# A hybrid decoder layer: the first SSD chunk is transposed by matmuls, and the probabilities of the last four head pairs by VectorE and DRAM

## The chip, the core and the metric

The kernel runs on one core of one Trainium2 chip. Five engines run side by side, each through its own instructions in order: PE (TensorE, matmuls; PEld is its loading of stationary operands), DVE (VectorE), ACT (ScalarE), POOL (GpSimd) and SP (SyncE, which here only starts DMAs). The metric is the device time of one execution in microseconds, as the median of several runs. Before the change it is 1031.97 us (three runs, 1031.74 to 1032.63).

## The reference, cut to what matters

One decoder layer over 512 tokens of width 1024, in float32. The token mixer projects the normalized input once and feeds two branches: attention with a window of 128 and a learned sink per head (16 query heads, 2 key heads), and a state-space scan (SSD) in chunks of 128 tokens (32 heads in 4 groups). Both are projected back, gated, summed and projected again; a SwiGLU block follows.

```python
# attention, in blocks of 128 queries against 256 keys (the block before and its own)
scores = einsum('bnqkgd,bnskd->bnkgqs', qb, k_band)
p = exp(where(valid, scores + bias, -inf) - m)
p = p / (sum(p, -1) + exp(sink - m))
out = einsum('bnkgqs,bnskd->bnqkgd', p, v_band)          # sums over the keys s
# SSD, one chunk c of 128 tokens, group g, head e
X = xh * dt[..., None]                                   # tokens x 64 per head
CB = einsum('bclgn,bcsgn->bcgls', Cc, Bc)
y_diag = einsum('bcgels,bcsgep->bclgep', exp(segsum(dA)) * CB, X)
states = einsum('bclgn,bcgel,bclgep->bcgepn', Bc, decay_states, X)
```

Both last sums run over tokens that the kernel holds along the wrong axis: the probabilities lie as queries x keys and the product with V wants keys on the partitions; x and B come out of the projection as channels x tokens, and the SSD products want tokens on the partitions. So both need 128x128 transposes.

## The kernel before, in words

All large products are made in three passes (`mm3`, lines 149 to 151: high x high, low x high, high x low parts of the operands), 24 matmuls of 128x512 per unit of 128 output columns. A unit's weights are loaded to `w_raw` (SP, line 120, four buffers), rounded to `w_hi` by ACT (line 135) and subtracted to `w_lo` by DVE (line 136), three units ahead; its result is taken out of one of three PSUM accumulators by ACT and DVE.

PE's order is the program's text. The side work (scores, transposes, SSD products) is written between calls of `fill(us)`, each of which lets a list of projection units go on for some steps of three matmuls. For DVE, ACT, POOL and SP the text does not fix the order: a scheduler places their instructions by its own estimate of when each can run, and from then on each engine takes them strictly in turn.

Attention, one pair of heads `t` (0 to 7) after the other. `scores(t+1)` makes the scores (line 436), the bias and mask (441, 443), the maximum (449), eight exps on ACT (461), the sums and reciprocal (463, 464), and POOL multiplies the reciprocal in (466): `sc`, two heads x four blocks of 128x256, of which 128 columns per block are stored, each block's own keys and the past block's sharing one square by the triangle mask. Then `weighted_values(t)` transposes the eight squares on PE (479, into `ps_pt`), and splits each by the triangle: the part at or before the query is `ps_pt` times `tri` on DVE (485), the rest is copied by ACT (481) and masked by POOL (482). Both make `pT`, the moving operand of `ps_o` (492).

The loop over `t` sits at lines 673 to 695. During the last pairs ACT also takes the exps' results on: sigmoids of `tB` (714) and SiLUs of the first group's x, B and C (716), with a table load of the activation function at each turn from one to the other. POOL multiplies and adds the input normalization's weights into four `row` tiles (704, 705) behind the last pair's mask. Then eight units `yb` follow.

SSD, 16 chunks `i` (4 groups x 4). `ssd_pre` loads the cumulative sums `L` by a broadcasting DMA, POOL masks them (756) and ACT takes 8 exps (761). `ssd_x` transposes x and B in squares of 32 on DVE (770, 781), writes them to DRAM (`t_d`, `b_d`) and reads them back with the squares in their places (`R`, `bt`; SP, lines 774 to 786). `ssd_dt` multiplies dt in: `X` on DVE (797), `Xd` on POOL (805). `ssd_a` makes C x B (822), copies it (824) and multiplies it into `L` (826). `ssd_b` makes the state `ps_st` (836), then `ps_yo` and `ps_yd` (862). Ahead of the loop stand `ssd_pre` of two chunks and the transposes of two; in it each step prepares the chunks after.

## Time and profile before

| | us |
|---|---|
| median of the runs shown | 1031.97 |
| the profiled execution | 1031.27 |
| its span, first to last instruction | 1029.5 |
| PE busy | 1008.2 (98% of the span) |
| DVE, ACT, POOL busy | 616.8, 499.2, 207.4 |
| largest wait of PE in one place | 10.0 |

An engine's line gives its busy time; the rows of 40 slices give it in tenths per slice of 25.7 us, and PEclk is the clock granted to TensorE. A timeline row gives start, length, engine, line, operation, output <- inputs, shape and count, and in brackets how long the engine stood idle before it and what ended that. A row of the chain of waits gives start, length and what ran. Matmuls of one stream overlap: 0.39 us is one's length, about 0.23 us the distance from one to the next.

### The profile page before, as it was taken

Reading aid. Unit: us, or ns where it says so; the run is one execution under the profiler, and the core shown is the slowest. Engines: PE = TensorE matmul, PEld = TensorE weight load, DVE = VectorE, ACT = ScalarE, POOL = GpSimd, SP = SyncE. Lnnn points to the kernel's source line nnn. Section 1 sums busy time; section 2 is a strip of 40 time slices with the busy share of each in tenths; the row PEclk is TensorE's granted clock in tenths of the full one; section 3 lists DMA queues with packets and bytes.
Section 4 is the critical chain, followed back from the end, with each engine's and each line's share of the span. In section 5 each row is a group of like instructions: output and inputs, shape, how many; then the busy total and the mean of one; then the engine's idle time right before and its main releaser. Section 6 shows DMA issues by size and latency. Waiting matters only on the chain.

```text
span 1029.5 us, 13358 instructions
## 1 busy us (share of the span) xinstructions
PE 1008.2 (98%) x4968; PEld 830.0 (81%) x4968; DVE 616.8 (60%) x911; ACT 499.2 (48%) x848; POOL 207.4 (20%) x195
## 2 busy tenths in 40 slices
PE   8999999996999999999999999999999999999997
PEld 7888888884887887888888888898888888888886
DVE  6789874545655785696874585646433333332766
ACT  5464566716555786684652543334323332322441
POOL 2011223722204113212322820290000000000000
PEclk9999999998999999999999999999999999999999
DMA  8211223545554445445532344316433333331471
GB/s 316 82 62 62 88 83 106 198 146 148 171 156 146 153 153 151 125 142 159 166 113 83 115 150 180 107 42 225 144 122 114 111 111 114 123 123 62 147 251 53
DMA packets 58961, 136.53 MB, mean 133 GB/s; under 512 B 12912, under 2 KB 23152, under 8 KB 58640
## 3 DMA queue, kind: packets, MB, share of 16 engines
q1 hardware_dynamic: 56240, 126.11, 37.9%
q0 software_dynamic: 2080, 7.47, 2.0%
q10 hardware_dynamic: 576, 2.10, 0.5%
q8 instruction: 39, 0.64, 0.3%
q14 instruction: 26, 0.21, 0.1%
HBM read 124.25 MB, written 11.40 MB: 132 GB/s over the span
## 4 chain that ended last, share of the span: by engine, by line
PE 88%; DVE 4%; ACT 3%; DMA 3%; issue 1%; POOL 1%; SPq 0%; ACTq 0%; POOLq 0%; DVEq 0%
PE ps_mm L149 13%; PE ps_mm L150 13%; PE ps_mm L151 13%; PE ps_ff L151 8%; PE ps_ff L149 8%; PE ps_ff L150 8%; PE ps_da L151 2%; PE ps_da L149 2%; PE ps_da L150 2%; PE ps_db L150 2%; PE ps_db L151 2%; PE ps_db L149 2%; PE ps_mix L149 1%; PE ps_mix L151 1%; PE ps_mix L150 1%; DMA L<-a_d 1%
## 5 line engine op out<-in xcount | busy, mean ns | idle before, releaser
L136 DVE TENSOR_TENSOR w_lo<-w_raw,w_hi 128x1024 fp32r<-128x1024 f32 x185 | 241.3, 1309 | 171.1 <-ACT w_hi L135 169.0
L135 ACT CAST w_hi<-w_raw 128x1024 fp32r<-128x1024 f32 x185 | 193.6, 1050 | 307.9 <-PE ps_ff L150 124.4
L149 PE MATMUL ps_mm<-hT_hi,w_hi 128*128 128x512 f32 x504 | 204.3, 405 | 0.7 <-DVE cacc L373 0.7
L150 PE MATMUL ps_mm<-hT_lo,w_hi 128*128 128x512 f32 x504 | 197.2, 391 | 0.0
L151 PE MATMUL ps_mm<-hT_hi,w_lo 128*128 128x512 f32 x504 | 197.0, 391 | 0.0
L149 PE MATMUL ps_ff<-h2T_hi,w_hi 128*128 128x512 f32 (+1 forms) x384 | 143.3, 373 | 0.0
L151 PE MATMUL ps_ff<-h2T_hi,w_lo 128*128 128x512 f32 (+1 forms) x384 | 142.6, 371 | 0.0
L150 PE MATMUL ps_ff<-h2T_lo,w_hi 128*128 128x512 f32 (+1 forms) x384 | 142.6, 371 | 0.0
L149 PEld LDWEIGHTS ps_mm<-hT_hi,w_hi 128*128 128x128 f32 x504 | 95.0, 188 | 23.2 <-issue 4.2
L151 PEld LDWEIGHTS ps_mm<-hT_hi,w_lo 128*128 128x128 f32 x504 | 94.8, 188 | 20.6
L150 PEld LDWEIGHTS ps_mm<-hT_lo,w_hi 128*128 128x128 f32 x504 | 95.1, 189 | 18.7 <-issue 1.2
L150 PEld LDWEIGHTS ps_ff<-h2T_lo,w_hi 128*128 128x128 f32 x384 | 72.3, 188 | 12.6
L151 PEld LDWEIGHTS ps_ff<-h2T_hi,w_lo 128*128 128x128 f32 x384 | 72.3, 188 | 12.5
L149 PEld LDWEIGHTS ps_ff<-h2T_hi,w_hi 128*128 128x128 f32 x384 | 72.3, 188 | 12.4
L1152 DVE TENSOR_TENSOR sgf<-sgf,ps_ff 128x512 f32<-128x512 f32 x22 | 15.1, 685 | 68.3 <-PE ps_ff L151 68.3
L149 PE MATMUL ps_mm<-yh,w_hi 128*128 128x512 f32 x124 | 49.4, 399 | 0.3 <-ACT yacc L934 0.3
L150 PE MATMUL ps_mm<-yl,w_hi 128*128 128x512 f32 x124 | 48.4, 390 | 0.0
L151 PE MATMUL ps_mm<-yh,w_lo 128*128 128x512 f32 x124 | 48.3, 390 | 0.0
L756 POOL TENSOR_SCALAR_AFFINE_SELECT L<-L 128x1024 f32<-128x1024 f32 x16 | 21.8, 1360 | 118.2 <-DMA L<-a_d 92.5
L761 ACT ACTIVATE L<-L,nac 128x128 f32<-128x128 f32 x128 | 40.1, 390 | 6.9 <-POOL L L756 6.6
L373 DVE SCALAR_TENSOR_TENSOR cacc<-ps_mm,pc,cacc 128x511 f32<-128x511 f32 (+2 forms) x54 | 39.6, 737 | 6.2 <-ACT cacc L370 5.7
L150 PE MATMUL ps_da<-w_lo,hA_hi 128*128 128x512 f32 x88 | 34.2, 389 | 0.0
(264 smaller groups left out, 1675.4 us busy)
## 6 DMA issues: line engine op xcount, KB each, us to landing
w_raw<-in_wall_dram SPq DMA_DIRECT2D x187, 512.0 KB, 3.4
L<-a_d SPq DMA_DIRECT2D x16, 512.0 KB, 5.9
t_d<-T SPq DMA_DIRECT2D x16, 256.0 KB, 3.9
R<-t_d SPq DMA_DIRECT2D x64, 64.0 KB, 2.0
E<-e_d SPq DMA_DIRECT2D x24, 128.0 KB, 3.5
x_d<-x_sb POOLq DMA_DIRECT2D x4, 512.0 KB, 7.8
row<-x_d POOLq DMA_DIRECT2D x4, 512.0 KB, 5.1
h_d<-row POOLq DMA_DIRECT2D x4, 512.0 KB, 3.0
```

The source lines that it names most:

```text
L135: (copy or nc.scalar.copy)(out=hi, in_=w)
L136: self.last = (eng or nc.vector).tensor_sub(out=lo, in0=w, in1=hi.bitcast(F32))
L149: nc.tensor.matmul(ps, lh, rh, start=start, stop=False)
L150: nc.tensor.matmul(ps, lh, rl, start=False, stop=False)
L151: nc.tensor.matmul(ps, ll, rh, start=False, stop=stop)
L373: nc.vector.scalar_tensor_tensor(out=acc[:, d:], in0=ps[:, :S - d], scalar=pc[:, cw + 3 - d:cw + 4 - d], in1=acc[:, d:], op0=ALU.mult, op1 ...
L756: nc.gpsimd.affine_select(out=Lf, in_=Lf, pattern=[[0, 8], [1, P]], compare_op=ALU.is_ge, fill=-BIG, base=0, channel_multiplier=-1)
L761: nc.scalar.activation(L[:, j, t], L[:, j, t], AF.Exp, bias=nac5[:, g, j, c, t:t + 1], scale=1.0)
L1152: nc.vector.tensor_mul(sg, sg, pu)
```

## The change

For the pairs 4 to 7 the eight transposes on PE go away. Instead DVE transposes in squares of 32 into `Tp`, one DMA writes 512 KB to DRAM (`p_d`), four DMAs of 128 KB read it back into the place of `sc`, and POOL and DVE multiply by `past` and `tri` into `pT`; ACT's copies for these pairs go away too. The writing half is issued behind `scores(t+1)`, the multiplications stand two yields ahead of `ps_o`. For the first SSD chunk the way over DRAM goes away: PE transposes x (`ps_x`) and B (`ps_bt`), `X` is made from `ps_x` in PSUM, and ACT copies `ps_bt`.

```diff
+    p_d = dram.tile([NQ, P, 4, 2 * P], F32, name="p_d")
...
+    def transposed_p(t):
+
+        sc = att_p[t]
+        T = Tp
+        if not back_t:
+            nc.gpsimd.tensor_sub(past, ones, tri)
+        for j in range(2):
+            nc.vector.transpose(
+                T[:, :, NT * j:NT * j + NT].rearrange("p b m s -> p m b s"),
+                sc[:, j].rearrange("p m (b s) -> p m b s", b=4))
+        nc.sync.dma_start(out=p_d[t], in_=T.rearrange("p b m s -> p b (m s)"))
+        back = sc.rearrange("p j n k -> p (j n k)").rearrange("p (a x) -> p a x", a=4)
+        for b in range(4):
+            nc.sync.dma_start(
+                out=back[32 * b:32 * b + 32], in_=p_d[t, :, b].rearrange("(a r) x -> r a x", r=32))
+        back_t[t] = back.rearrange("p a (m s) -> p m a s", s=32)
...
     def weighted_values(t):
...
-        for j in range(2):
+        if t in back_t:
+            yield
+            for j in range(2):
+                own = back_t[t][:, NT * j:NT * j + NT]
+                last_sel[0] = nc.gpsimd.tensor_tensor(
+                    out=pT[:, j, 1::2].rearrange("p n (a s) -> p n a s", a=4), in0=own[:, 1:],
+                    in1=past.rearrange("p (a s) -> p a s", a=4).unsqueeze(1).broadcast_to([P, NT - 1, 4, 32]),
+                    op=ALU.mult)
+                nc.vector.tensor_tensor(
+                    out=pT[:, j, 0::2].rearrange("p n (a s) -> p n a s", a=4), in0=own,
+                    in1=tri.rearrange("p (a s) -> p a s", a=4).unsqueeze(1).broadcast_to([P, NT, 4, 32]),
+                    op=ALU.mult)
+            yield
+        for j in range(0 if t in back_t else 2):
             ps = axt([P, NT, P], "ps_pt")
...
+    past = at.tile([P, P], F32, name="past")
+    Tp = at.tile([P, 4, 2 * NT, 32], F32, name="Tp")
...
             next(s1)
+            if t + 1 >= NQ // 2:
+                transposed_p(t + 1)
...
+    def ssd_first():
+
+        ps = axt([P, 4, P], "ps_x")
+        for t in range(4):
+            nc.tensor.transpose(ps[:, t], xbc_t[0, 2 + t][:, 0:P], ident)
+        R_t[0] = ps.rearrange("p t (a s) -> p a t s", a=4)
+        ps = axt([P, P], "ps_bt")
+        nc.tensor.transpose(ps, xbc_t[0, 0][:, 0:P], ident)
+        bt_t[0] = sd.tile([P, P], F32, name="bt", tag="bt", bufs=2)
+        nc.scalar.copy(out=bt_t[0], in_=ps)
...
     ssd_pre(0)
     ssd_pre(1)
-    ssd_x(0)
     ssd_a(0)
-    fill(4.0)
+    ssd_first()
     ssd_dt(0)
     ssd_x(1)
+    fill(4.0)
```

The list of units is empty at both places of `fill(4.0)` (the units of the SSD stage are added inside the loop), so moving it moves nothing.

The scheduled engines change order at three places. First, DVE at the last pair, from its sums to the end of its output. Before:

```order
L463 TENSOR_TENSOR sm<-sm,es 128x8
L464 RECIPROCAL sm<-sm 128x8
L136 TENSOR_TENSOR w_lo<-w_raw,w_hi 128x1024
L231 TENSOR_TENSOR attT_lo<-ps_o,attT_hi 128x512
L136 TENSOR_TENSOR w_lo<-w_raw,w_hi 128x1024
L485 TENSOR_TENSOR pT<-ps_pt,tri 128x4x128 x2
L136 TENSOR_TENSOR w_lo<-w_raw,w_hi 128x1024
L231 TENSOR_TENSOR attT_lo<-ps_o,attT_hi 128x512
```

And now:

```order
L464 TENSOR_TENSOR sm<-sm,es 128x8
L465 RECIPROCAL sm<-sm 128x8
L136 TENSOR_TENSOR w_lo<-w_raw,w_hi 128x1024
L481 STREAM_TRANSPOSE Tp<-sc 128x4x4x32 x2
L231 TENSOR_TENSOR attT_lo<-ps_o,attT_hi 128x512
L136 TENSOR_TENSOR w_lo<-w_raw,w_hi 128x1024 x2
L504 TENSOR_TENSOR pT<-sc,tri 128x4x128 x2
L231 TENSOR_TENSOR attT_lo<-ps_o,attT_hi 128x512
```

The two multiplications into `pT` stood behind the second `w_lo` after the reciprocal; now they stand behind the third.

Second, ACT in the same stretch, from the copy behind the last pair's exps to the `w_hi` that belongs to that third `w_lo`. Before:

```order
L411 COPY tB<-ps_mm 128x512
L135 CAST w_hi<-w_raw 128x1024
L714 ACT_TABLE_LOAD
L714 ACTIVATE tB<-tB 128x512
L481 COPY pT<-ps_pt 128x3x128 x2
L716 ACT_TABLE_LOAD
L716 ACTIVATE bc_f<-bc_f 128x512
L411 COPY tB<-ps_mm 128x512
L135 CAST w_hi<-w_raw 128x1024
```

And now:

```order
L135 CAST w_hi<-w_raw 128x1024
L412 COPY tB<-ps_mm 128x512
L754 ACT_TABLE_LOAD
L754 ACTIVATE bc_f<-bc_f 128x512
L752 ACT_TABLE_LOAD
L752 ACTIVATE tB<-tB 128x512
L754 ACT_TABLE_LOAD
L754 ACTIVATE bc_f<-bc_f 128x512
L412 COPY tB<-ps_mm 128x512
L135 CAST w_hi<-w_raw 128x1024
```

The two copies into `pT` are gone; the first `w_hi` has moved ahead of a table load and a SiLU that came before it; the last `w_hi` has the same work ahead of it as before, without the copies.

Third, ACT at the start of SSD. Before:

```order
L824 COPY cb<-ps_cb 128x128 x2
L761 ACT_TABLE_LOAD
L761 ACTIVATE L<-L,nac 128x128 x16
L370 ACTIVATE cacc<-ps_mm,pc 128x512
L135 CAST w_hi<-w_raw 128x1024
L761 ACTIVATE L<-L,nac 128x128 x8
```

And now:

```order
L873 COPY cb<-ps_cb 128x128
L837 COPY bt<-ps_bt 128x128
L873 COPY cb<-ps_cb 128x128
L799 ACT_TABLE_LOAD
L799 ACTIVATE L<-L,nac 128x128 x24
L371 ACTIVATE cacc<-ps_mm,pc 128x512
L135 CAST w_hi<-w_raw 128x1024
L891 COPY h_st<-ps_st 128x512
```

The exps of the third `L` have moved ahead of the first unit's evacuation (`cacc`) and of a `w_hi`.

## The prediction

> **What bounds the kernel now.** I read the page first, then PE's waits, then PE's timeline where it waits. The engines' busy time, and their shares of the chain of waits:

> ```profile
> PE 1008.2 (98%) x4968; PEld 830.0 (81%) x4968; DVE 616.8 (60%) x911; ACT 499.2 (48%) x848; POOL 207.4 (20%) x195
> PE 88%; DVE 4%; ACT 3%; DMA 3%; issue 1%; POOL 1%; SPq 0%; ACTq 0%; POOLq 0%; DVEq 0%
> ```

> PE bounds it: 98% busy, 88% of the chain. The longest of its waits (total, times, longest):

> ```profile
> PE ps_st L836 <- POOL Xd L805: 10.0, 1, 10.0
> ```

> So apart from this one, about half of the 2% that PE idles, only instructions taken off PE can gain, and any new wait of PE costs in full. The change does both, at two places.

> **First place: the start of SSD.** PE's timeline around the wait (start, length), a normal `ps_st` and the transposes' rate from the chain of waits, and the clock by windows (its column is the last but two):

> ```profile
> 244.06 0.39 PE L150 MATMUL ps_mm<-hT_lo,w_hi 128*128 128x512 f32 x1
> 244.28 0.39 PE L151 MATMUL ps_mm<-hT_hi,w_lo 128*128 128x512 f32 x1
> 254.64 2.08 PE L836 MATMUL ps_st<-Xd,bt 128*128 128x512 f32 x2 [9.97 <-POOL Xd L805]
> 258.52 0.40 PE L151 MATMUL ps_mm<-hT_hi,w_lo 128*128 128x512 f32 x1
> 277.46 0.86 PE ps_st L836 x2
> 646.92 0.44 PE ps_tr L217 x4
> 247.00:248.00 1.00, 0.00 (x0) 0.00 (x0) 0.30 (x2) 0.92 (x4) 0.05 (x1) 1.00 0.71 258
> 248.00:249.00 1.00, 0.00 (x0) 0.00 (x0) 1.00 (x2) 1.00 (x5) 0.00 (x0) 0.55 0.45 139
> 258.00:259.00 1.00, 1.00 (x5) 0.76 (x5) 0.00 (x0) 0.00 (x0) 1.00 (x3) 0.83 0.35 84
> ```

> From 244.28 to 258.52 pass 14.24 us. The work in between is one `ps_st` (0.86) and six steps from one matmul to the next (0.23 each), some 2.35 with the turns. So the place costs 11.9: 10 of waiting and 1.9 because the clock fell 3.4 us into the idle time and came back 3.7 us after PE had work. What PE waited for is the chain over DRAM and then a busy DVE:

> ```profile
> 238.05 0.88 DVE L770 STREAM_TRANSPOSE T<-xs_f 128x128 f32<-128x128 f32 x4
> 238.18 2.56 ACT L819 ACTIVATE y_g<-xs_f,pc 128x512 f32<-128x512 f32 x4
> 241.43 5.92 DMA b_d<-Tb
> 252.79 0.75 DVE L797 TENSOR_TENSOR X<-R,dtv 128x256 f32<-128x256 f32 x2
> 253.29 1.30 POOL Xd L805 x2
> ```

> The change removes this way for the first chunk. `X` needs only `ps_x` (PE, right ahead of the fill) and DVE, free at 238.05; two `X` (0.75) and two `Xd` (1.3, ahead of the masks on POOL now) end near 241, `bt` behind ACT's four `y_g` (to 240.7) near 241, and `ps_st` is due at 245. That is four us of cover; gone, each us of it is PE's. Added on PE: five transposes at 0.11, 0.55. **Gain 11.9 - 0.55 = 11.3.**

> What is late next: PE is 11 us earlier against ACT and DVE, and ACT now takes all 24 exps before it empties the first unit's accumulator.

> ```profile
> 251.83 2.45 ACT L761 ACTIVATE L<-L,nac 128x128 f32<-128x128 f32 x8 [0.70 <-POOL L L756]
> 249.44 0.76 ACT L370 ACTIVATE cacc<-ps_mm,pc 128x512 f32<-128x512 f32 x1
> 247.93 1.18 DVE L826 TENSOR_TENSOR L<-L,cb 128x1024 f32<-128x1024 f32 x1
> 249.91 1.89 POOL L756 TENSOR_SCALAR_AFFINE_SELECT L<-L 128x1024 f32<-128x1024 f32 x1 [2.86 <-DMA L<-a_d]
> ```

> The third `L` landed at 249.9; with 256 KB (`t_d` of the first chunk) less ahead of it, moved at about 260 KB per us by the window row above, and an issue earlier (0.3), it lands some 1.3 earlier and the exps, which ended at 254.3, end near 253.0. `cacc` 0.76, then DVE's three additions (0.7 each) with a `w_lo` (1.2, as the product in the third row) among them: free near 257.1. PE wants that accumulator for its fourth unit at 245.1 + 0.9 (`ps_st`) + nine steps of 0.68 + 1.1 (`ps_yd`) + five steps = 256.6. **Loss 0.5**; none if `L` lands 0.5 earlier still, 1.8 if it lands as before. `ps_yd` itself needs the first `L`, whose product ended at 249.1 before: three us of cover.

> **Second place: the transposes off PE.** PE's timeline in pair 5 (`ps_pt` is a group of four transposes):

> ```profile
> 147.00 0.48 PE L149 MATMUL ps_mm<-hT_hi,w_hi 128*128 128x512 f32 x1
> 147.78 0.60 PE L479 MATMUL ps_pt<-ident,sc 128*128 128x128 f32 x4
> 148.14 0.48 PE L149 MATMUL ps_mm<-hT_hi,w_hi 128*128 128x512 f32 x1
> ```

> From step to step pass 1.14 with a group, and three distances, 0.68, without: 0.46 a group, eight groups. **Gain 3.7**, if `pT` is there in time. ACT loses four pairs of copies, off the path.

> The new way of pair 5, by rows: DVE's reciprocal, POOL's `sc`, the write (512 KB as `w_raw`), four reads (`R`'s issue time and landing), the multiplication on DVE, and `ps_o` of pairs 4 and 5; the transposes are in the row at 238.05 (four of 128x128 stand for one half):

> ```profile
> 136.49 0.20 DVE L464 RECIPROCAL sm<-sm 128x8 f32<-128x8 f32 x1
> 136.84 2.04 POOL L466 TENSOR_TENSOR sc<-sc,sm 128x512 f32<-128x512 f32 x2 [3.64 <-DVE sm L464]
> w_raw<-in_wall_dram SPq DMA_DIRECT2D x3, 512.0 KB, 3.3
> 247.47 1.75 SPq L776 DMA_DIRECT2D R<-t_d  x4
> R<-t_d SPq DMA_DIRECT2D x8, 64.0 KB, 2.1
> 179.99 1.29 DVE L485 TENSOR_TENSOR pT<-ps_pt,tri 128x512 f32<-128x512 f32 x2 [1.08 <-ACT pT L481]
> 138.17 1.73 PE L492 MATMUL ps_o<-pT,v_sb 128*64 128x256 f32 x16
> 154.46 1.74 PE L492 MATMUL ps_o<-pT,v_sb 128*64 128x256 f32 x16
> ```

> 138.9 + 0.9 + 3.4 + 1.75 + 2.1 = 147.0 on landing; the four multiplications, one after another, 2.8 more (POOL three quarters of 1.02, DVE 0.65, twice each): 149.8, wanted at 154.46 - 1.84 = 152.6. Pairs 4 and 6 come out with 2.8 to 2.9 to spare in the same way. The `w_raw` that SP holds behind these reads wait for a `w_lo` that ends later still.

> Pair 7 is different, by the order of DVE and ACT. Its `pT` stand behind a third `w_lo`, and that behind a `w_hi` at the end of ACT's table loads:

> ```profile
> 168.79 0.57 ACT L411 COPY tB<-ps_mm 128x512 f32<-128x512 f32 x1
> 179.49 0.84 ACT L481 COPY pT<-ps_pt 128x384 f32<-128x384 f32 x2
> 182.65 1.05 ACT L135 CAST w_hi<-w_raw 128x1024 fp32r<-128x1024 f32 x1
> 184.45 1.74 PE L492 MATMUL ps_o<-pT,v_sb 128*64 128x256 f32 x16
> ```

> ACT works from 168.79 to 183.70 without a gap; the same instructions less the copies are 14.07. They start 1.84 earlier (four groups of PE) and 0.6 earlier (DVE now makes the maxima `nm` of this pair ahead of pair 6's `pT`, 0.65 one), so at 166.35: `w_hi` ends at 180.4. `ps_o` is wanted at 184.45 - 3.7 = 180.8. Behind 180.4 come `w_lo` (1.2, as `L`'s product, of the same size and also from two SBUF operands) and two `pT` (1.29): 182.9, 2.1 late. And POOL is in the way, with `row` right behind its own half of `pT`:

> ```profile
> 183.64 2.37 POOL L705 TENSOR_TENSOR row<-row,gb 128x1024 f32<-128x1024 f32 x1
> 183.73 3.36 DVE L136 TENSOR_TENSOR w_lo<-w_raw,w_hi 128x1024 fp32r<-128x1024 f32 x1 [2.46 <-ACT w_hi L135]
> 185.97 3.39 POOL L704 TENSOR_TENSOR row<-row,gb 128x1024 f32<-128x1024 f32 x1
> 188.08 0.69 DVE L231 TENSOR_TENSOR attT_lo<-ps_o,attT_hi 128x512 fp32r<-128x512 f32 x1 [0.99 <-ACT attT_hi L230]
> ```

> A `w_lo` took 3.36 instead of 1.2 when it met `row`, and the next `row` took a us longer: they take turns. `attT_lo`, which reads PSUM, ran at full speed beside one. The new `pT` on DVE reads two SBUF operands like `w_lo`. In this pair the exps end at 166.35; 0.5 for the sums, pair 5's 10.2 from `sc` to landing, and a us for `sc`'s own turn behind a `w_lo` give 178.1; POOL's `pT` end at 179.7 and `row` follows. So 2.4, 1.2 and 1.3 come one after another, from 179.7 to 180.4 on, and end at 184.6 to 185.3. **Loss 4.2**, from 2.1 (no turn lost) to 5.3 (POOL's second half falls in between too). The clock fell after 3.4 us of idling above; whether it falls here hangs on one us, so of 0 to 1.9 I take **1.0**.

> [...]

> **Sum.** Against the profiled execution, 1031.27: - 11.3 + 0.5 - 3.7 + 4.2 + 1.0 = 1022.0. The median is 0.7 above that execution: **1022.7 us**.

> **Rivals.**

> *No wait at pair 7* (20%). If ACT or DVE run ahead of my sum by 2 us and the turn goes the other way, both gains stay: 1031.97 - 15.0 + 0.5 = 1017.5. For it: PE waits nowhere in attention now. Against: the order is fixed, and ACT has no gap in that stretch to lose.

> *The wait moves at SSD* (11%). The third `L` lands later than before, since it now competes with the reads of the second chunk at once; each us of it goes to PE through `cacc`. At 3 us later than before: 1022.7 + 1.8 - 0.5 + 3 = 1027.0. Against: 256 KB less are moved.

> *The SSD start gains nothing* (5%): another input of `ps_st` or `ps_yd` is as late as `Xd` was. For it: `b_d`, 64 KB, took 5.9 here, and the second chunk's now stands in its place. Then 1022.7 + 11.3 = 1034, or about the time before if pair 7 is in time.

> *The round trips are all late, slower than before* (4%). `pT(t)` stands ahead of the next pair's sums on DVE, so a late trip delays the next trip. The ring is sums 0.4, `sc` 2.0, transposes 0.9, write 3.5, reads 3.85, `pT` 2.8 = 13.5 against PE's 15.4 per pair (154.46 - 138.17, less two groups). With every trip x longer, pair 4 waits x - 2.8 and three more x - 1.9 each: 4x - 8.5. That eats the 15 us from x = 5.9 on; at 7 it is 19.5, and the time 1036.5. For it: 64 KB (`b_d`) took 5.9 in the crowd at SSD's start. Against: between 160 and 182 `w_raw`, four times as large, took 3.3.

> **How the numbers follow.** The forecast has 60%, its own range 1019.5 (2.1 late, no clock) to 1025.5 (5.3, clock 1.9, SSD 1.0). With the rivals on both sides 8 in 10 lie from 1017 to 1027.5. A difference of 0.2%, 2 us, is what a measurement tells here. Faster: 60 + 20 + 11 and a part of the 5, 92%; same 4%; slower 4%.

> **What would show it.** Right: `ps_st` is gone from PE's waits; `ps_o` stands there once, 3 to 5 us, on DVE `pT` near 181 us, with `w_lo` just ahead of it and a `row` beside; `ps_pt` counts 32. PE waits under 1 us on `cacc` or `w_lo` near 257. Wrong: `ps_o` waiting in pairs 4 to 6 or on a DMA, no wait at pair 7, or PE idle at 245 to 256 for another reason.

## The result

The changed kernel takes 1025.83 us (median of four runs, 1025.16 to 1026.41) against 1031.86 us before (four runs beside it, 1031.68 to 1032.63): a ratio of 0.994, with a 95% interval of 0.992 to 0.996. It is 6.0 us faster. The forecast was 1022.7 us. The time lies inside the outer range of 1017 to 1027.5 and just above the forecast's own, 1019.5 to 1025.5; 3.1 us of the gain are missing. The profiled execution took 1025.5 us, and its span is 1023.8 us where it was 1029.5.

The engines' busy time on the page of the changed kernel, and the longest of PE's waits (total, times, longest):

```profile
PE 1006.9 (98%) x4941; PEld 828.5 (81%) x4941; DVE 625.7 (61%) x914; ACT 492.9 (48%) x839; POOL 211.3 (21%) x196
```

```profile
PE ps_o L525 <- DVE pT L504: 4.5, 1, 4.5
PE ps_o L525 <- DVE sm L464: 0.8, 1, 0.8
PE ps_o L525 <- POOL pT L500: 0.7, 1, 0.7
```

The wait for `Xd`, 10 us, is gone, and the one for `pT` that was forecast at pair 7 is there with 4.5. The other two are at pair 6, and the forecast did not have them. PE's timeline of the changed kernel puts each in its place:

```profile
137.03 1.73 PE L525 MATMUL ps_o<-pT,v_sb 128*64 128x256 f32 x16
152.38 2.37 PE L525 MATMUL ps_o<-pT,v_sb 128*64 128x256 f32 x16
168.48 0.65 PE L525 MATMUL ps_o<-pT,v_sb 128*64 128x256 f32 x2 [0.71 <-POOL pT L500]
169.88 1.73 PE L525 MATMUL ps_o<-pT,v_sb 128*64 128x256 f32 x14 [0.75 <-DVE sm L464]
171.54 0.50 PE L149 MATMUL ps_mm<-hT_hi,w_hi 128*128 128x512 f32 x1
187.87 3.82 PE L525 MATMUL ps_o<-pT,v_sb 128*64 128x256 f32 x16 [4.48 <-DVE pT L504]
191.62 0.57 PE L149 MATMUL ps_mm<-hT_hi,w_hi 128*128 128x512 f32 x1
250.64 1.02 PE L885 MATMUL ps_st<-Xd,bt 128*128 128x512 f32 x2
257.76 1.09 PE L911 MATMUL ps_yd<-L,X 128*64 128x128 f32 x16
```

The same last stretch before, from the step behind pair 7's `ps_o` to `ps_yd`:

```profile
186.11 0.50 PE L149 MATMUL ps_mm<-hT_hi,w_hi 128*128 128x512 f32 x1
263.63 1.09 PE L862 MATMUL ps_yd<-L,X 128*64 128x128 f32 x16
```

That stretch took 77.52 us and takes 66.14: 11.4 gained at the SSD start. A `ps_o` in time has 1.73 in its row and lets the next step begin 1.66 after its own start. Pair 4 loses nothing. Pair 5's row is 0.64 longer. Pair 6 starts 0.78 late and takes 3.06 to the next step, so it loses 2.2. Pair 7 starts 4.55 late and takes 3.75 to the next step, so it loses 6.6. Together:

| place | forecast, us | measured, us |
|---|---|---|
| SSD start, with `cacc` | -11.3 + 0.5 | -11.4 |
| eight groups of transposes off PE | -3.7 | -3.7 |
| pairs 5 and 6 | 0 | +2.8 |
| pair 7, with the clock | +4.2 + 1.0 | +6.6 |
| sum | -9.3 | -5.7 |

The spans differ by 5.7 too. So there are two questions: why pairs 5 and 6 were late, and what pair 7's 6.6 is made of.

**Pairs 5 and 6.** The DMA view of the changed kernel in two windows, 141 to 149 and 157 to 167 us (issues, KB each, median us to landing):

```profile
sc<-p_d SPq DMA_DIRECT2D x4, 128.0 KB, 5.5
gb<-in_ln_in_dram POOLq DMA_DIRECT2D x1, 512.0 KB, 5.8
...
sc<-p_d SPq DMA_DIRECT2D x4, 128.0 KB, 4.7
gb<-in_ln_in_dram POOLq DMA_DIRECT2D x1, 512.0 KB, 6.7
```

A `gb` of 512 KB (the weights for `row`), issued on POOL's queue, moves beside the reads of each of these pairs: in the two windows the packets of its queue took 19.8% and 17.5% of the 16 DMA engines' time, those of SP's 58.9% and 63.7%. The loads were there before too, at nearly the same times, and nothing waited for the transfers beside them then (POOL's timeline of the kernel before):

```profile
145.04 0.59 POOL L698 DMA_DIRECT2D gb<-in_ln_in_dram  x1 [6.16 <-PE ps_sc L436]
161.32 0.61 POOL L698 DMA_DIRECT2D gb<-in_ln_in_dram  x1 [4.93 <-PE ps_sc L436]
```

Pair 6's reads were issued from 159.12 us on and the last landed near 166.9. Then the halves of `pT` take turns (DVE and POOL of the changed kernel):

```profile
166.88 2.10 DVE L504 TENSOR_TENSOR pT<-sc,tri 128x512 f32<-128x512 f32 x2 [3.27 <-DMA sc<-p_d]
168.90 0.95 DVE L464 TENSOR_TENSOR sm<-sm,es 128x8 f32<-128x8 f32 x1
166.99 2.84 POOL L500 TENSOR_TENSOR pT<-sc,past 128x384 f32<-128x384 f32 x2 [6.50 <-DMA sc<-p_d]
```

POOL's second half is done at 169.83, and PE goes on at 169.88 (its row names `sm`, which ended in the same instant). Behind `pT` on DVE stand the sums of pair 7: `sm`, eight columns, took 0.95, to the end of POOL's half, where it took 0.17 at pair 4, and the last trip starts late.

**Pair 7** (ACT, DVE and POOL of the changed kernel, and three windows around the end of PE's wait, where the clock is the last column but two):

```profile
171.65 0.59 ACT L230 CAST attT_hi<-ps_o 128x512 fp32r<-128x512 f32 x1 [1.51 <-PE ps_o L525]
182.08 1.05 ACT L135 CAST w_hi<-w_raw 128x1024 fp32r<-128x1024 f32 x1
183.17 1.80 DVE L136 TENSOR_TENSOR w_lo<-w_raw,w_hi 128x1024 fp32r<-128x1024 f32 x1 [6.49 <-ACT w_hi L135]
184.90 3.43 DVE L504 TENSOR_TENSOR pT<-sc,tri 128x512 f32<-128x512 f32 x2
181.92 1.98 POOL L500 TENSOR_TENSOR pT<-sc,past 128x384 f32<-128x384 f32 x2 [8.82 <-DMA sc<-p_d]
183.85 3.33 POOL L742 TENSOR_TENSOR row<-row,gb 128x1024 f32<-128x1024 f32 x1
```

```profile
187.00:188.00 1.00, 0.13 (x1) 0.16 (x2) 1.00 (x2) 0.53 (x2) 0.18 (x1) 1.00 0.62 250
188.00:189.00 1.00, 1.00 (x6) 0.43 (x7) 0.33 (x1) 0.00 (x0) 0.14 (x1) 0.69 0.02 8
191.00:192.00 1.00, 1.00 (x4) 0.60 (x3) 0.00 (x0) 0.27 (x1) 0.84 (x1) 0.60 0.76 307
```

The forecast's chain is there link by link: `w_hi` at the end of ACT's table loads, the third `w_lo`, and `pT` in turns with `row`. Everything stands 2.7 to 3.8 us later than forecast (`w_hi` ends at 183.1, not 180.4; the trip lands near 181.9, not 178.1), and PE itself is 2.5 later than forecast when it wants `pT` (183.3, not 180.8). `w_hi` is late because ACT, which the forecast had without a gap, stood idle for pair 6's late `ps_o` (1.51, the first row) and then 0.56 for PE's next unit. And the clock is halved from 188.4 to 191.8, when PE is already at work again.

### The profile page after: what moved, and what is told of

It reads as the page before. It is cut to its first block, busy times and chain, and to the rows that moved or that the text cites. A ratio compares the mean times of both kernels' runs of the same rounds, so it can differ in the third digit from the quotient of the medians.

```text
span 1023.8 us, 13323 instructions
## 1 busy us (share of the span) xinstructions
PE 1006.9 (98%) x4941; PEld 828.5 (81%) x4941; DVE 625.7 (61%) x914; ACT 492.9 (48%) x839; POOL 211.3 (21%) x196
## 4 chain that ended last, share of the span: by engine, by line
PE 87%; DVE 4%; DMA 3%; ACT 2%; issue 1%; POOL 1%; SPq 0%; POOLq 0%; DVEq 0%; ACTq 0%
PE ps_mm L149 13%; PE ps_mm L150 13%; PE ps_mm L151 13%; PE ps_ff L150 8%; PE ps_ff L151 8%; PE ps_ff L149 8%; PE ps_da L150 2%; PE ps_da L151 2%; PE ps_da L149 2%; PE ps_db L150 2%; PE ps_db L149 2%; PE ps_db L151 2%; PE ps_mix L149 1%; PE ps_mix L151 1%; PE ps_mix L150 1%; PE ps_yd L911 1%
## 5 line engine op out<-in xcount | busy, mean ns | idle before, releaser
L135 ACT CAST w_hi<-w_raw 128x1024 fp32r<-128x1024 f32 x185 | 193.4, 1051 | 307.7 <-PE ps_ff L150 120.7
L136 DVE TENSOR_TENSOR w_lo<-w_raw,w_hi 128x1024 fp32r<-128x1024 f32 x185 | 236.9, 1285 | 155.2 <-ACT w_hi L135 153.0
L149 PE MATMUL ps_mm<-hT_hi,w_hi 128*128 128x512 f32 x504 | 202.8, 402 | 0.7 <-DVE cacc L374 0.7
L150 PE MATMUL ps_mm<-hT_lo,w_hi 128*128 128x512 f32 x504 | 196.8, 390 | 0.0
L151 PE MATMUL ps_mm<-hT_hi,w_lo 128*128 128x512 f32 x504 | 196.6, 390 | 0.0
L149 PE MATMUL ps_ff<-h2T_hi,w_hi 128*128 128x512 f32 (+1 forms) x384 | 143.2, 373 | 0.0
L150 PE MATMUL ps_ff<-h2T_lo,w_hi 128*128 128x512 f32 (+1 forms) x384 | 142.6, 371 | 0.0
L151 PE MATMUL ps_ff<-h2T_hi,w_lo 128*128 128x512 f32 (+1 forms) x384 | 142.6, 371 | 0.0
L149 PEld LDWEIGHTS ps_mm<-hT_hi,w_hi 128*128 128x128 f32 x504 | 94.8, 188 | 23.4 <-issue 4.5
L151 PEld LDWEIGHTS ps_mm<-hT_hi,w_lo 128*128 128x128 f32 x504 | 94.6, 188 | 20.3
L150 PEld LDWEIGHTS ps_mm<-hT_lo,w_hi 128*128 128x128 f32 x504 | 94.8, 188 | 18.5 <-issue 1.0
L149 PEld LDWEIGHTS ps_ff<-h2T_hi,w_hi 128*128 128x128 f32 x384 | 72.3, 188 | 12.6
L150 PEld LDWEIGHTS ps_ff<-h2T_lo,w_hi 128*128 128x128 f32 x384 | 72.3, 188 | 12.5
L151 PEld LDWEIGHTS ps_ff<-h2T_hi,w_lo 128*128 128x128 f32 x384 | 72.3, 188 | 12.4
L149 PE MATMUL ps_mm<-yh,w_hi 128*128 128x512 f32 x124 | 49.4, 398 | 0.2 <-ACT yacc L983 0.2
L150 PE MATMUL ps_mm<-yl,w_hi 128*128 128x512 f32 x124 | 48.3, 390 | 0.0
L151 PE MATMUL ps_mm<-yh,w_lo 128*128 128x512 f32 x124 | 48.3, 390 | 0.0
L794 POOL TENSOR_SCALAR_AFFINE_SELECT L<-L 128x1024 f32<-128x1024 f32 x16 | 18.4, 1147 | 78.1 <-DMA L<-a_d 68.3
L149 PE MATMUL ps_da<-w_hi,hA_hi 128*128 128x512 f32 x88 | 34.2, 389 | 0.0
## 6 DMA issues: line engine op xcount, KB each, us to landing
w_raw<-in_wall_dram SPq DMA_DIRECT2D x187, 512.0 KB, 3.5
L<-a_d SPq DMA_DIRECT2D x16, 512.0 KB, 5.6
x_d<-x_sb POOLq DMA_DIRECT2D x4, 512.0 KB, 7.8
p_d<-Tp SPq DMA_DIRECT2D x4, 512.0 KB, 2.8
```

The costliest lines, as they stand in the source:

```text
L135: (copy or nc.scalar.copy)(out=hi, in_=w)
L136: self.last = (eng or nc.vector).tensor_sub(out=lo, in0=w, in1=hi.bitcast(F32))
L149: nc.tensor.matmul(ps, lh, rh, start=start, stop=False)
L150: nc.tensor.matmul(ps, lh, rl, start=False, stop=False)
L151: nc.tensor.matmul(ps, ll, rh, start=False, stop=stop)
L794: nc.gpsimd.affine_select(out=Lf, in_=Lf, pattern=[[0, 8], [1, P]], compare_op=ALU.is_ge, fill=-BIG, base=0, channel_multiplier=-1)
```

## The experiments

Each is an edit of the changed kernel, with the kernel before measured beside it. The kernels of different rows were not all measured side by side, and the runs of one spread over 0.5 to 3.3 us, so a difference of one us between rows says little by itself; the traces have to bear it out. Medians:

| run | us | ratio to before, 95% |
|---|---|---|
| the change | 1025.8 | 0.992 to 0.996 |
| SSD part alone | 1020.4 | 0.988 to 0.991 |
| attention part alone | 1036.1 | 1.003 to 1.006 |
| `gb` later | 1024.6 | 0.992 to 0.995 |
| pair 7 by PE | 1019.9 | 0.987 to 0.990 |
| `row` later | 1025.4 | 0.992 to 0.996 |
| PE kept at work | 1025.7 | 0.992 to 0.995 |
| `pT` first | 1019.9 | 0.986 to 0.989 |
| `gb` later, pair 7 by PE | 1019.1 | 0.986 to 0.989 |
| `gb` last, `pT` first | 1020.6 | 0.988 to 0.991 |
| DVE alone | 1022.3 | 0.989 to 0.992 |
| pairs 1 to 5 | 1023.4 | 0.991 to 0.993 |
| pairs 4 and 5 | 1017.8 | 0.984 to 0.988 |

**The two parts apart.**

```diff
# SSD part alone
-            if t + 1 >= NQ // 2:
+            if False:
                 transposed_p(t + 1)
# attention part alone
+    ssd_x(0)
     ssd_a(0)
-    ssd_first()
+    fill(4.0)
     ssd_dt(0)
     ssd_x(1)
-    fill(4.0)
```

> Only the SSD part; attention as before, so all eight pairs by PE. Theory (the two parts are separate, and the SSD part gains what its place shows): from the normal ps_o of the last pair to ps_yd the changed kernel is 11.4 us shorter than the one before, so 1031.9 - 11.4 = 1020.5, and no wait for Xd, and none near 245 to 265. Rival (the gain at SSD is owed in part to attention's end coming late, which gives the masks' loads and L time): 3 us or more of a wait at ps_yd or cacc, 1023.5 or more.

> Only the attention part; SSD starts as before. Theory (pairs 5 and 6 lose 2.8, pair 7 loses 6.6, the eight groups of transposes give 3.7, and SSD's wait of 10 us stays): 1031.9 + 5.7 = 1037.6, slower than before. Rival (SSD's wait absorbs it, because what it waits for does not move with PE): about 1032.

The SSD part alone gives 11.5 us, as its place showed, and PE waits nowhere between 236 and 300. Against it, the whole change is 5.4 us slower: the attention part costs more than it gives. Alone it is 4.2 slower than before, with PE's wait for `Xd` still 9.8. It was expected 5.7 slower: in its profiled execution pairs 5 and 6 lost 0.2 and 0.6 only, and pair 7 5.8. So the loss at pairs 5 and 6 is not the same in each execution (0.9 here, 2.8 in the change), and the two parts add up to within 1.2 us (-11.5 + 4.2 against -6.0).

**The `gb` loads.**

```diff
+            if t == 6:
+                sel_6[0] = last_sel[0]                   # POOL's pT of pair 6
...
     for i, t in enumerate(gb1):
-        nc.gpsimd.dma_start(out=t, in_=ln_in[i:i + 1].broadcast_to([P, D]))
+        with tc.issue_after(sel_6[0].ins):
+            nc.gpsimd.dma_start(out=t, in_=ln_in[i:i + 1].broadcast_to([P, D]))
```

> The changed kernel with the two 512 KB loads of gb issued after POOL's pT of pair 6 instead of at 143.9 and 159.9 us, beside the reads of pairs 5 and 6. Theory A (these loads share the DMA engines with the reads and make them 5.5 and 6.4 us instead of the 3 of pairs 4 and 7): the reads of pairs 5 and 6 land in 3 to 3.5 us, ps_o waits in neither pair, 2.8 us gained, 1023.0; pair 7 waits as long as now, since ACT's and DVE's order there is the same. Rival B (DVE's and POOL's halves of pT take turns, and that alone makes pairs 5 and 6 late): under 1 us gained, 1025. Rival C (the w_raw that SP loads around the reads are the crowd): the reads still take 5 us or more and the time stays.

The reads in the same two places (DMA view, windows 141 to 149 and 157 to 167 us):

```profile
sc<-p_d SPq DMA_DIRECT2D x4, 128.0 KB, 3.7
...
sc<-p_d SPq DMA_DIRECT2D x4, 128.0 KB, 3.3
```

They fell from 5.5 and 4.7 to 3.7 and 3.3, pair 5 lost nothing and pair 6 1.2 instead of 2.2. The other traces agree: from the issue of the first read to the start of `pT` on the landing pairs 5 and 6 took 7.4 and 7.8 us in the change and pair 6 took 6.3 in the run of the attention part alone, with a `gb` beside them, and pair 6 took 4.8 in the run with `gb` last and `pT` first. So theory A is right of the reads, and rival C, which had the `w_raw` loads at fault, falls. Theory A is not right that pair 6 would then lose nothing, and the median came down by 1.2, not 2.8, no more than the spread of the runs.

Two things took the rest. First, with the reads in time, POOL's `pT` of pair 5 ran beside pair 6's `nm` and `es` on DVE (DVE of this run; in the change the two took 0.16 and 0.17):

```profile
149.48 0.98 DVE L452 TENSOR_TENSOR nm<-nm,nsnk 128x8 f32<-128x8 f32 x1
150.50 0.94 DVE L455 TENSOR_TENSOR es<-nm,snk 128x8 f32<-128x8 f32 x1
```

The exps wait for these, so pair 6's sums came 1.3 us later against PE than in the change, and its `pT` still took turns with POOL's: what stays at pair 6 is rival B's turns, as far as the trace shows. Second, the loads now stood beside pair 7's write (SP and POOL):

```profile
174.64 0.33 SPq L484 DMA_DIRECT2D p_d<-Tp  x1
180.26 1.79 SPq L487 DMA_DIRECT2D sc<-p_d  x4
...
185.40 2.90 POOL L500 TENSOR_TENSOR pT<-sc,past 128x384 f32<-128x384 f32 x2 [12.55 <-DMA sc<-p_d]
```

From the write's issue to the reads' passed 5.6 us, where it was 3.1 (173.87 to 176.96 in the changed kernel), and the trip landed at 185.4, not 181.9; pair 7 lost 7.2. Moving a crowd moves the wait.

**Pair 7 by PE.**

```diff
-            if t + 1 >= NQ // 2:
+            if NQ // 2 <= t + 1 < 7:
                 transposed_p(t + 1)
```

> The changed kernel with pair 7 transposed by PE as before; pairs 4 to 6 go through DRAM. Theory (pair 7's loss of 6.6 is its own): it goes, the two groups of transposes cost 0.9 again, 1025.8 - 5.7 = 1020.1, with the small waits of pairs 5 and 6 unchanged. Rival (pair 6's lateness is handed on through ACT, whatever way pair 7 takes): ps_o of pair 7 still waits 2 us or more, 1022 or more.

1019.9: the 6.6 are pair 7's own and vanish with its trip, though pair 6 still loses its 2.2 (`ps_o` at 168.01, the step behind it at 171.07).

With both edits:

> Pairs 4 to 6 through DRAM with the gb loads behind pair 6's pT, pair 7 by PE. In the run with only the gb loads moved, the reads of pairs 5 and 6 fell to 3.7 and 3.3 us, pair 5 lost nothing and pair 6 1.2, and the loads slowed pair 7's write instead (5.6 us). Theory (without pair 7's trip nothing is left for them to slow): pair 5 loses nothing, pair 6 about 1.2 as there, pair 7 nothing: 1019.9 - 1.4 = 1018.5. Rival (the loads now slow w_raw or row, and a w_lo or ps_o of pair 7 waits): 1020 or more.

1019.1, 0.6 over what was expected and 0.7 under the run above, which is less than either spreads. Pair 5 loses nothing, pair 6 1.4.

**What pair 7's loss is made of.** Three edits, one link each. `row` later: a copy of one column of `attT_hi` to a new tile stands ahead of `row` on POOL, so that `row` starts behind `ps_o`.

```diff
+        if ti == 0:
+            seen = at.tile([P, 1], F32, name="seen")
+            last_sel[0] = nc.gpsimd.tensor_copy(seen, attT_hi.bitcast(F32)[:, NQ - 1, 0:1])
         with tc.issue_after(last_sel[0].ins):
             nc.gpsimd.tensor_mul(row, row, gb1[0])
```

> The changed kernel with POOL's row products and sums held until attT_hi of pair 7 is written, so nothing of POOL but its own halves of pT runs beside DVE's w_lo and pT of pair 7. Theory (the row of 3.33 us at 183.85 takes turns with w_lo and pT): w_lo back to 1.2, the two pT to 1.3 together, ps_o of pair 7 waits 2 us instead of 4.5, and as that is under the 3.4 us after which the clock fell, it also runs at full speed: 2.5 + 2.1 gained, 1021.2. Rival (ACT's late w_hi and the landing at 181.9 decide, and the turn only fills time that is lost anyway): the wait stays above 4 us, about 1025.

The timeline of this run, DVE's `pT`, PE's `ps_o`, and two steps of the product that follows:

```profile
183.50 2.08 DVE L504 TENSOR_TENSOR pT<-sc,tri 128x512 f32<-128x512 f32 x2
...
185.13 3.63 PE L525 MATMUL ps_o<-pT,v_sb 128*64 128x256 f32 x16 [2.92 <-DVE pT L504]
...
199.80 0.40 PE L149 MATMUL ps_mm<-attT_hi,w_hi 128*128 128x512 f32 x1
200.04 0.40 PE L150 MATMUL ps_mm<-attT_lo,w_hi 128*128 128x512 f32 x1
```

The turn is as the theory has it: without `row` the two `pT` take 2.08, not 3.43 (the first still meets POOL's half), and the wait falls from 4.5 to 2.9. But the clock fell all the same, to half from 185.0 to 188.4 and after only 2.9 us of idling, so `ps_o` took 3.56 to the next step, not 1.66. Pair 7 loses 4.9 instead of 6.6. Yet the median gained only 0.4. This build differs in one more thing, which takes back some of the gain: in the eight units that read `attT`, the distance from step to step is 0.2334 us where it is 0.2267 in the change, and 192 of them cost 1.3. Why was not tried; the new tile of one column in `attT`'s pool, and the copy that writes it, are what the other kernels lack.

PE kept at work:

```diff
+        if t == 7:
+            ps = axt([P, P], "ps_w")
+            for _ in range(28):
+                nc.tensor.transpose(ps, ident, ident)
         ps = axt([P, S], "ps_o")
```

> The changed kernel with 28 transposes of the identity on PE, into a PSUM tile that nothing reads, just ahead of ps_o of pair 7, so that PE works for 3 us of its wait. Theory (the clock fell in the wait and makes ps_o take 3.75 us to the next step instead of 1.67): the wait for pT ends at the same time, ps_o takes 1.7 again, 2.1 gained, 1023.7. Rival (ps_o is slow because its operands come late one after another, at any clock): no gain, 1025.8.

The timeline of this run on PE and DVE, and one window with the clock:

```profile
183.62 3.22 PE L524 MATMUL ps_w<-ident 128*128 128x128 f32 x28
186.76 0.65 PE L529 MATMUL ps_o<-pT,v_sb 128*64 128x256 f32 x2
189.38 2.80 PE L529 MATMUL ps_o<-pT,v_sb 128*64 128x256 f32 x14 [1.97 <-DVE pT L504]
...
184.98 4.25 DVE L504 TENSOR_TENSOR pT<-sc,tri 128x512 f32<-128x512 f32 x2
```

```profile
189.00:190.00 1.00, 0.62 (x6) 0.56 (x8) 0.23 (x1) 0.00 (x0) 0.24 (x1) 0.90 0.00 0
```

Neither side was right. `row` came between DVE's two `pT` this time (4.25 for both), so the wait split, and 1.97 us of idling in its second half were enough to halve the clock, from 189.8 to 193.2. The run did not isolate the clock's price, but it shows that idling need not last 3.4 us. With the transposes the clock stayed up: from 183.6 to 186.8 PE had nothing else, and the clock was at 1.00.

`pT` first: DVE makes pair 7's `pT` ahead of the third `w_lo`. For this the multiplications of pair 7 also stand one yield earlier in the text; on DVE, POOL and ACT nothing else changes place up to pair 7's `ps_o`.

```diff
+            if t == 7:
+                units.hold = pT_dve.ins                  # set behind the two pT of pair 7
...
+                if self.hold:
+                    with tc.issue_after(self.hold):
+                        self.last = nc.vector.tensor_sub(out=lo, in0=w, in1=hi.bitcast(F32))
```

> The changed kernel with one thing moved: on DVE, the two pT of pair 7 stand ahead of the third w_lo instead of behind it. Theory (pT waits for w_lo, not for its data, which land at 181.9): pT takes turns with POOL's halves only, ends near 184.8, ps_o waits 1.5 us, the clock stays, 1025.8 - 3 - 2.1 = 1020.7; w_lo then meets the row and is 3 us later, for a unit that PE starts only after another 5. Rival (that w_lo is due at once): the wait goes to ps_mm, 1023 or more.

DVE and PE at pair 7 in the timeline of this run:

```profile
181.29 2.12 DVE L509 TENSOR_TENSOR pT<-sc,tri 128x512 f32<-128x512 f32 x2 [4.75 <-DMA sc<-p_d]
183.33 2.01 DVE L138 TENSOR_TENSOR w_lo<-w_raw,w_hi 128x1024 fp32r<-128x1024 f32 x1
...
183.19 0.65 PE L534 MATMUL ps_o<-pT,v_sb 128*64 128x256 f32 x2
184.32 1.73 PE L534 MATMUL ps_o<-pT,v_sb 128*64 128x256 f32 x14 [0.48 <-POOL pT L505]
```

The place of `pT` on DVE is the cause that counts: 5.9 us for the two `pT` moved ahead of one `w_lo`, 0.8 more than expected. Pair 7 loses 1.1, the clock stays at 1.00, and nothing waits for the `w_lo` that now stands behind.

**Both causes mended, all four pairs kept.** The edit above, and the `gb` loads behind POOL's last `pT`:

```diff
     for i, t in enumerate(gb1):
+        with tc.issue_after(last_sel[0].ins):
             nc.gpsimd.dma_start(out=t, in_=ln_in[i:i + 1].broadcast_to([P, D]))
```

> All four pairs through DRAM, with pair 7's pT on DVE ahead of the third w_lo, and the gb loads issued behind POOL's last pT, so that they meet no trip. Theory (the losses of the changed kernel are the gb loads beside the trips and the order at pair 7, and nothing more than the turns of the two halves of pT is left): pair 5 loses nothing, pair 6 about 1.3, pair 7 about 1.3, against 0.6, 2.2 and 6.6: 1025.8 - 6.8 = 1019.0, 0.9 under the run with the order alone. Rival (something else makes pairs 6 and 7 late): no better than 1019.9.

1020.6, where 1019.0 was expected: no better than the edit alone. The four runs fall in two pairs, 1019.4 and 1021.9, and the profiled one, 1021.98, is of the slower pair; what the faster two did is not on record. In the profile pairs 5 and 6 lose 0 and 0.5 now, and pair 7 4.7 (DVE and PE in the timeline of this run):

```profile
168.82 2.85 DVE L140 TENSOR_TENSOR w_lo<-w_raw,w_hi 128x1024 fp32r<-128x1024 f32 x1 [0.93 <-ACT w_hi L135]
171.59 1.29 DVE L485 STREAM_TRANSPOSE Tp<-sc 128x512 f32<-128x512 f32 x2
...
182.88 0.65 PE L534 MATMUL ps_o<-pT,v_sb 128*64 128x256 f32 x2 [1.69 <-POOL pT L505]
184.28 3.25 PE L534 MATMUL ps_o<-pT,v_sb 128*64 128x256 f32 x14 [0.76 <-POOL pT L505]
```

PE now comes to pair 7 2.1 us earlier than in the run before (180.80 for its last step, not 182.87), but the trip lands at the same 181.3. A `w_lo` in turns with POOL's `sc` (2.85 where it takes 1.2 alone) stands ahead of the transposes, so the write starts only 0.8 earlier (172.91, not 173.72); and from it to the reads' issue pass 3.9 instead of 2.9, beside a `w_raw` issued 1.2 ahead of it. The time that pair 6 lost had been pair 7's cover. And the clock fell once more, to half from 184.0 to 187.4, after two pieces of idling (1.7 and 0.8).

**DVE alone makes `pT`.** Pair 7 by PE and the `gb` loads last, as above, and:

```diff
-                last_sel[0] = nc.gpsimd.tensor_tensor(
+                nc.vector.tensor_tensor(
                     out=pT[:, j, 1::2].rearrange("p n (a s) -> p n a s", a=4), in0=own[:, 1:],
```

> Pairs 4 to 6 through DRAM with all of pT made by DVE, none by POOL; pair 7 by PE, gb loads behind its pT. Theory (what is left of pair 6's loss, 1.4 in the run with the gb loads moved and pair 7 by PE, is DVE and POOL taking turns, which makes the last half of pT 2.8 us late and sm 0.95 long): four multiplications of 0.5 and 0.65 on DVE alone take 2.3, sm 0.2, so pair 6 loses 0.5: 1019.1 - 0.9 = 1018.2. Rival (the reads' landing is late by itself): 1019 or more.

1022.3, worse. The scheduler moved pair 7's sums ahead of pair 6's `pT`, so POOL's `sc` of pair 7 ran beside DVE's `pT`, which took 1.39 and 1.52 for the second head instead of the first one's 0.56 and 0.64; pair 6 lost 3.3. The turns only changed partners. At the first head's lengths the four would take 2.4, near the 2.3 that was expected. The run says nothing of the landing.

**Pairs 1 to 5**, with 0, 6 and 7 by PE and the `gb` loads last:

```diff
-            if t + 1 >= NQ // 2:
+            if 1 <= t + 1 < 6:
                 transposed_p(t + 1)
```

> Pairs 1 to 5 through DRAM instead of 4 to 7, gb loads behind pair 7's pT, pairs 0, 6 and 7 by PE. Theory (a trip fits a pair's 15.4 us wherever no other transfer of 512 KB is issued beside its reads, and DVE has room): five pairs gain 0.93 each, 1020.4 - 4.6 = 1015.8. Rival (DVE carries dt's chain and the q halves in pairs 1 to 3, so that sums or pT come late there, and PE waits): 1019 or more.

1023.4, and the rival was right. In pair 1, DVE's second `pT` stood behind the sums and transposes of pair 2 and a step of dt's chain (DVE and PE in the timeline of this run):

```profile
90.17 0.68 DVE L504 TENSOR_TENSOR pT<-sc,tri 128x512 f32<-128x512 f32 x1
...
91.00 2.73 PE L525 MATMUL ps_o<-pT,v_sb 128*64 128x256 f32 x14 [3.33 <-DVE pT L504]
```

Pair 1 lost 5.0: behind the 3.33 its last 14 matmuls took 2.66 to the next step, which take 1.66 behind a wait of 2.05 in the run before. Pair 3 lost 2.1.

**Pairs 4 and 5 only**, with the first `gb` behind POOL's `pT` of pair 5:

```diff
-            if t + 1 >= NQ // 2:
+            if 4 <= t + 1 < 6:
                 transposed_p(t + 1)
...
     for i, t in enumerate(gb1):
+        with tc.issue_after(sel_5[0].ins):               # POOL's pT of pair 5
             nc.gpsimd.dma_start(out=t, in_=ln_in[i:i + 1].broadcast_to([P, D]))
```

> The SSD part, with only pairs 4 and 5 through DRAM and the first gb load behind POOL's pT of pair 5, so that no gb load stands beside their reads; pairs 6 and 7 by PE. Theory (these two trips end in time when nothing else is loaded beside them, as pair 4's did in the changed kernel and pair 5's in the runs with gb moved): two pairs gain 0.93 each and nothing is lost: 1020.4 - 1.9 = 1018.5, under both kernels and under every other run. Rival (a pair's gain is lost again behind it, on DVE or at SSD): 1019.5 or more.

1017.8 (three runs, 1016.5 to 1018.2; a fourth took 2105 us, for a reason that is not known, and is left out), the fastest of all, 14 us under the kernel before and 8 under the change. PE waits for no `ps_o`; pair 5's reads took 3.9.

## Why the prediction came out as it did

**The SSD start** was right. POOL's `Xd` in the changed kernel:

```profile
244.33 1.18 POOL L854 TENSOR_TENSOR Xd<-X,dec 128x256 f32<-128x256 f32 x2 [26.03 <-DVE X L846]
```

It is done at 245.5, five us ahead of `ps_st` at 250.64, where the forecast had four; the gain is 11.4 in the spans and 11.5 in the run of this part alone, against 11.3.

**The 0.5 at `cacc`** came out as 0, inside its 0 to 1.8. The order is as told: ACT took all 24 exps first. In the run of the SSD part alone the first unit's last addition ended near 255.8, and PE, five steps behind `ps_yd`, wanted its accumulator at 256.3: 0.5 to spare, where the forecast was 0.5 short.

**The transposes** were right: pair 4, where nothing else happened, gained 0.93, two groups at 0.46.

**Pairs 4 to 6 with "2.8 to 2.9 to spare"** is the step that failed for pairs 5 and 6. It took the reads' 3.85, from the first issue to the last landing, from `R`. That was too little for two reasons. `R`'s reads are of 64 KB and these of 128 KB: even with no `gb` beside them pair 6's took 4.8 in the run with `gb` last, and in the run with `gb` later pair 5 had 0.7 to spare (DVE's `pT` ended at 152.64, `ps_o` began at 153.33). And the forecast asked only what stands behind the reads on SP, not what POOL's queue sends at the same time. The `gb` rows stood in the trace of before at 145.04 and 161.32, inside the very stretches in which the forecast had the reads; beside them the reads took 6.3 to 7.8. Pair 4, which has no `gb`, was in time. The 2.8 for the four multiplications in turns was right (POOL's took 2.84).

**Pair 7's 4.2** had the right mechanism: the order on DVE, ACT's `w_hi` and the turn with `row`. Moving `pT` ahead of `w_lo` took 5.9 us off, and holding `row` cut the two `pT` from 3.43 to 2.08. The size was off by 0.3 in the wait alone (4.55), though in part by luck: the forecast had `row` ahead of `w_lo`, and in the trace `w_lo` met POOL's `pT` (1.80) and `pT` met `row` (3.43). What was missing was the link from pair 6 to pair 7. It has two arms. `pT` of pair 6 stands ahead of pair 7's sums on DVE, so the lateness of one trip is passed to the next, and the landing came at 181.9 instead of 178.1; and ACT waits for pair 6's `ps_o` ahead of `w_hi`, which ended at 183.1 instead of 180.4. The second arm set the wait, since the third `w_lo` started on `w_hi`; as PE was late by 2.5 itself, the wait grew by 0.3 only. The forecast had the first arm in its fourth rival, as a thing of all pairs, and left it out of the sum.

**The clock's 1.0** was mis-sized: it cost 2.1 (`ps_o` took 3.75 to the next step instead of 1.66). That "whether it falls here hangs on one us" rested on the 3.4 us of idling ahead of the fall at SSD, and the runs show falls after 2.0 to 2.9 us too. More on that below.

**The signs and the rivals.** The forecast's signs of being right came at SSD and at pair 7, but `ps_o` waiting in pair 6 was among its signs of being wrong, and it came too. No wait at pair 7: no. The wait moving at SSD: no. The late ring, given 4%, came true in part, as 2.8 us at two pairs and not as 19.5 at four. No rival had pairs 5 and 6 late by themselves, so that the outer range still held is partly luck: a loss that was on no list fitted into the room left for others. (The upper end of the forecast's own range comes out of its own terms as 1025.2, not 1025.5.) The sum was 3.6 too low by the table (2.8 at pairs 5 and 6, 1.4 at pair 7, less 0.6 at SSD); the median's distance of 3.1 is smaller since the profiled executions lie 0.3 to 0.6 under their medians.

## What to carry to other kernels

When a transfer is put on the path, look at every queue that sends in the same stretch and not only at the issuing one: here a load that nobody had waited for became a cause (reads of 5.5 and 4.7 us to landing beside it, 3.7 and 3.3 without). A stall that is mended gives its time to the next one, so price a chain of trips with the cover that is left when the ones before are in time. And check where a new instruction comes in its engine's order before costing it: one place on DVE was worth more here than all the work taken off PE, 5.9 us against 3.7.

## What the runs showed of the hardware

**The clock fell and returned on a grid, after a stretch that was mostly idle.** From windows of 0.1 us in seven runs, each end placed by the mean clock of the window that it falls in:

| run | clock halved | length | PE idle in the 3.4 us ahead |
|---|---|---|---|
| before, SSD start | 248.11 to 258.35 | 10.24 | 3.4 |
| the change, pair 7 | 188.39 to 191.80 | 3.41 | 2.9 |
| attention alone, pair 7 | 186.09 to 189.51 | 3.41 | 3.4 |
| `gb` later | 185.40 to 192.23 | 6.83 | 2.6 |
| `row` later | 185.02 to 188.43 | 3.41 | 2.8 |
| PE kept at work | 189.81 to 193.22 | 3.41 | 2.0 |
| `gb` last, `pT` first | 184.02 to 187.43 | 3.41 | 2.2 |

**Turns between DVE and POOL touched short instructions too.** `sm`, eight columns, took 0.17 us at pair 4 of the change and 0.95 at pair 6, beside POOL's `pT`. The four multiplications, which took 1.28 on DVE and 1.99 on POOL at pair 7 of the attention part alone, one engine after the other, took 2.10 and 2.84 side by side at pair 6 of the change.

**The distance between matmuls changed as a whole in one build.** With `row` later every step of one product took 0.2334 us instead of 0.2267, at a granted clock of 1.00. The cause is open.
